# Layer-1 U gathers of a two-layer PEER trunk tied to TensorE steps, and input rows loaded once

## The chip, the cores and the metric

One core of one Trainium2 chip runs the whole program. The metric is device time in microseconds (us) of one execution, given as the median of several runs. PE is TensorE, PEld its weight loads, DVE is VectorE, ACT is ScalarE, POOL is GpSimd, and SP issues the plain DMAs.

## The reference

The program is a two-layer decoder trunk on 512 tokens of width 1024. Layer 0 mixes tokens with sliding-window attention, layer 1 with a short gated convolution. After each mixer comes a PEER block: a router picks 128 of 16384 experts for every token (8 heads, 16 each), and each expert is a row of U and a row of V.

```
h = rmsnorm(x, norm_mix[i]);  x = x + mixer_i(h)          # attention in layer 0, gated conv in layer 1
h = rmsnorm(x, norm_ffn[i]);  x = x + peer_ffn(h, ...)
# peer_ffn, for each token t and each of its 128 experts k:
u = take(expert_u, idx);  a = einsum('td,thkd->thk', h, u)
w = g * gelu(a)
v = take(expert_v, idx);  y = einsum('thk,thkd->td', w, v)
```

## The kernel before, in words

The 512 tokens are four tiles of 128. The PEER block is done in two ways at once. For tiles 0 and 1 the expert rows are **gathered**: `gather(l, t, r)` (lines 622 to 690) issues 128 indirect DMAs for the U rows (line 633, one 512 KB tile `ug` each, one expert of every token), VectorE multiplies each with the normalised tokens and sums it (line 638), and when all 128 sums are there, 128 indirect DMAs fetch the V rows (line 666, `vg`, one token each), which TensorE multiplies with the weights into `acc` (line 676). The buffers are six tiles of the pool `gp`, and two more in the second front (`GX1`, line 74). POOL issues these DMAs in order; one waits there until its buffer is free.

For tiles 2 and 3 the block is **dense**: `dense(l, rs, pool)` (lines 692 to 788) goes over all 128 groups of 128 experts. Step i has a U half, `ustep` (line 704): load `du`, split it into a high and a low part (`uh` on ACT, `ul` on DVE, lines 700 and 701), 24 matmuls by `mm3` into `psA`, GELU into `dw`; and a V half, `vstep` (line 714): multiply `dw` with the gate matrix G (line 717, on POOL while U rows are being gathered, else on DVE), split `dv` and `dw` (`vh`, `vl`, `wh`, `wl`), and 12 matmuls into `y` (line 735). U halves run 7 steps ahead, 15 of them before the first V half, so that the first and the last 8 V steps have no U half beside them. G is built 32 groups at a time from one-hot matrices by 16 calls of `gen` (lines 738 to 762: copies `jr`, `igr` on ACT, `oj`, `igr`, `oi` on DVE, 32 pairs of small matmuls `psG`).

A **front** is what comes ahead of the dense steps of a layer. The second front (layer 1) is: add the dense sums to the rows of tiles 2 and 3 (`finish`, line 790), norms and transposes of tiles 1 to 3, `conv` (line 352; 24 pieces of weights, each split into `whi` and `wlo` and followed by 24 matmuls into `psbcu`), the output projection `proj`, and `router` (16 weight pieces, matmuls `psrq` and `psrs`, then top-k selection in many small instructions on DVE). Then come 15 U halves and the first 16 calls of `gen`, called the preparation below.

Three generators write the program: `stream_d` (fronts and dense steps), `stream_g` (the four gathers: layer 0 tiles 0 and 1, layer 1 tiles 0 and 1) and `stream_f` (work of tiles 0 and 1 in the gaps). `merge` (line 814) takes from them by a clock of its own: each `yield` says how far its stream moves on, and `rate()` (line 806) gives that step for one gather from `FR0`, `FR1` (fronts) and `DR0`, `DR1` (dense steps; first number for U rows, second for V rows); a dense step counts `DSTEP` = 6.8. The order so written sets priorities, from which a scheduler fixes one order for each engine. `st["mark"]` names a matmul; a U gather that is written while it is set waits for that matmul on POOL (line 635). Before, it is set in the attention of tiles 1 to 3 alone and is removed afterwards.

```
def rate():
    u = 0 if st.get("gu") else 1
    if st["dense"]:
        return (DR1 if "f1" in st else DR0)[u]
    if st["front"]:
        return (FR1 if "f0" in st else FR0)[u]
    return GR0
```

The rows of x: tile 0 is loaded at line 112, tiles 1 to 3 for their norm in `attn_norm` (line 223, pool `b4`), and all four again at the end of `attn` (line 349, pool `l0`), for the residual.

Of the kernel before, what the change touches and what calls it, by code (L numbers as in the profile page):

```python
# [8 lines left out]
F32 = mybir.dt.float32  # L9
# [10 lines left out]
P = 128  # L20
D = 1024
KC = 8
S = 512
NT = 4
# [48 lines left out]
WSB = 2  # L73
GX1 = 2

DR0 = (2.4, 2.4)
DR1 = (2.5, 2.5)
FR0 = (2.2, 3.0)
FR1 = (3.0, 3.0)


@with_exitstack
def trunk(ctx: ExitStack, tc: tile.TileContext, a: dict, out: bass.AP):
    nc = tc.nc
# [3 lines left out]
    b4 = ctx.enter_context(tc.tile_pool(name="b4", bufs=BPB))  # L88
# [20 lines left out]
    xs = {}  # L109
    first = {}  # L110
# [63 lines left out]
    def mm3(ps, w, x, ts):  # L174
        for k in range(KC):
            nc.tensor.matmul(ps, w[0][:, k, :], x[0][:, k, ts], start=(k == 0), stop=False)  # L176
            nc.tensor.matmul(ps, w[0][:, k, :], x[1][:, k, ts], start=False, stop=False)  # L177
        for k in range(KC):
            nc.tensor.matmul(ps, w[1][:, k, :], x[0][:, k, ts], start=False, stop=(k == KC - 1))  # L179

    def proj(src, lhs, tiles, psum, sp):
        for h in range(2):
# [32 lines left out]
    def attn_norm(tiles, pool):  # L215
        gain = first.pop("gain", None) or gain_of(a["norm_mix"][0:1, :])
        res = []
        for t in tiles:
            if "x" in first:
                xs[t] = first.pop("x")  # L220
            else:
                xs[t] = b4.tile([P, D], F32, name="xq", tag="b4")
                nc.sync.dma_start(xs[t], a["x"][t * P:(t + 1) * P, :])
            hT = pool.tile([P, KC, P], F32, name="hTa", tag="hTa", bufs=4)
            normT(t, gain, hT, py)
            res.append(hT)
        return res
# [17 lines left out]
    def attn(tiles, qks, pool, L):  # L245
# [5 lines left out]
        for j, t in enumerate(tiles):  # L251
# [22 lines left out]
            ps = py("psk")  # L274
# [22 lines left out]
            for gp2 in range(2):  # L297
# [46 lines left out]
                nc.scalar.copy(oT[:, gp2], psov)  # L344
                if sp:
                    nc.vector.tensor_tensor(oL[:, gp2], psov, oT[:, gp2], op=ALU.subtract)
        for t in tiles:
            xs[t] = pool.tile([P, D], F32, name="x", tag="x", bufs=3)
            nc.sync.dma_start(xs[t], a["x"][t * P:(t + 1) * P, :])
        yield from proj(a["wo"], oTs, tiles, py, (pool, ("sc", "sc"), SCB) if sp else None)  # L350

    def conv(tiles, pool, psum, slow=1.0):
        n = len(tiles)
        T = n * P
# [36 lines left out]
        for c in range(KC):  # L391
            pss = [None] * 3
            cc = pool.tile([P, 3, T + 2], F32, name="cc", tag="cc")
            u, z, v = cc[:, 0, :T], cc[:, 1, :], cc[:, 2, :T]
            for part in (2, 1, 0):
                w = piece(a["w_in"][c, part])
                ps = psum(f"psbcu{part}")
                if c3:
                    mm3(ps[:, :T], split(w, pool, ("wh", "wl"), WSB), (hh, hl), slice(0, T))
                else:  # L400
                    for k in range(KC):
                        nc.tensor.matmul(ps[:, :T], w[:, k, :], hT[:, k, :], start=(k == 0), stop=(k == KC - 1))
                if part == 2:
                    nc.scalar.copy(u, ps[:, :T])
                elif part == 1:
                    nc.vector.tensor_copy(z[:, 0:2], zh[:, c, :])
                    nc.vector.tensor_tensor(z[:, 2:], ps[:, :T], u, op=ALU.mult)
                    nc.vector.tensor_copy(zh[:, c, :], z[:, T:T + 2])
                    nc.scalar.mul(v, z[:, 0:T], convw[:, 0, c:c + 1])
                    for q in (1, 2):  # L410
                        nc.vector.scalar_tensor_tensor(v, z[:, q:T + q], convw[:, q, c:c + 1], v,
                                                       op0=ALU.mult, op1=ALU.add)
                else:
                    y = v if sp else yT[:, c, :]
                    nc.vector.tensor_tensor(y, v, ps[:, :T], op=ALU.mult)
                    if sp:
                        nc.scalar.copy(yh[:, c, :], y)
                        nc.vector.tensor_tensor(yl[:, c, :], y, yh[:, c, :], op=ALU.subtract)
                yield 1.75 * n * slow
# [202 lines left out]
    def gather(l, t, r):  # L622
# [5 lines left out]
        for s in range(P):  # L628
            if early and s % TK == 0:
# [2 lines left out]
            ug = gtile("ug")  # L632
            ld = nc.gpsimd.indirect_dma_start(out=ug, out_offset=None, in_=a[f"u{l}"],  # L633
                                              in_offset=bass.IndirectOffsetOnAxis(ap=r["idx"][h][:, c:c + 1], axis=0))
            if "mark" in st:
                tc.add_manual_dep(ld.ins, st["mark"], together, reason="pace of the front")
            with tc.high_priority(offset=HPT):
                nc.vector.tensor_tensor_reduce(out=ug, in0=ug, in1=xn, scale=1.0, scalar=0.0, op0=ALU.mult,  # L638
# [53 lines left out]
    def dense(l, rs, pool):  # L692
# [21 lines left out]
        def vstep(i):  # L714
# [17 lines left out]
            for k, (x, m) in enumerate(terms):  # L732
                for tt in range(2):
                    for h in range(2):
                        nc.tensor.matmul(ys[tt][h], x[:, tt * P:(tt + 1) * P], m[:, h * 512:(h + 1) * 512],  # L735
                                         start=first and k == 0, stop=last and k == len(terms) - 1)

        def gen(i, tg):
            ijg = rs[tg * TG // P]["ijg"]
# [29 lines left out]
                gen(c * IC, tg)  # L769

        npre = GR - IC
        for i in range(LAG + npre):
            ustep(i)
            yield 1.0
# [3 lines left out]
        for i in range(NK):  # L778
# [7 lines left out]
            vstep(i)  # L786
            yield DSTEP
        st["ys"] = ys

    def finish(l, ys, pool):  # L790
        for tt in range(2):
# [70 lines left out]
    def stream_d():  # L862
        with tc.tile_pool(name="l0", bufs=1) as l0:
# [28 lines left out]
            def run(g):  # L892
                for v in g:
                    if isinstance(v, list):
                        return v
                    yield v
            hTs = attn_norm([0], l0)
            yield 5.0
            qk0 = yield from run(attn_qkv([0], hTs, l0, L, py, piece, 1.75))
            hTs = attn_norm([1, 2, 3], l0)  # L900
# [92 lines left out]
```

## Time and profile before

| what | value |
|---|---|
| median of 3 runs | 2992.05 us (2991.13 to 2999.46) |
| the profiled execution, its own time | 2989.34 us |
| its span, first to last instruction | 2987.5 us |
| busy, share of the span | PE 88%, PEld 70%, DVE 75%, ACT 52%, POOL 46% |
| mean granted TensorE clock | 0.943 |
| moved by DMA | 931.37 MB, mean 312 GB/s |

The 40 slices of the page, 75 us each, show the stages; each digit is the busy share in tenths. Counted from 0, the second front begins in slice 22 and the dense V steps of layer 1 in slice 28.

```profile
PE   5966878869999988999998699986788699999999
...
DVE  2496699984898899546479995988999946546655
...
POOL 0152554464555545434357754446755755541000
PEclk8987889969999999999999799998899899999999
```

PE is the engine with the most work, and the shares differ from stage to stage: there are slices in which DVE is at 9 and PE at 6 to 8, and the last eight have PE at 9, DVE near 5 and POOL falling to 0, which is where the gathers have ended. Below, a stage is named by its window in us from the start of the span, and a dense step of layer 1 by its number from 0 to 127.

### The profile page before, as it was taken

The numbers are of one execution on the slowest core, as the hardware profiler recorded it, in microseconds if no ns is written. First come the engines' busy times: TensorE is split into PE (matmuls) and PEld (weight loads), VectorE is DVE, ScalarE is ACT, GpSimd is POOL, SyncE is SP. The second block draws the span as 40 slices with busy tenths as digits, with TensorE's granted clock in tenths as the row PEclk, the third lists the DMA queues.
The fourth block names the chain that finished last, engine by engine and source line by source line (L and its number), as shares of the span: only waits on it lengthen the run. The fifth ranks groups of instructions, "written<-read, shape, count | busy, mean of one in ns | idle before, by whom it ended". The sixth has DMA issues, their size and how long they took to land. (4 is left out here: it accounts for less than half of the span.)

```text
span 2987.5 us, 53454 instructions
## 1 busy us (share of the span) xinstructions
PE 2624.3 (88%) x19980; PEld 2098.1 (70%) x19980; DVE 2246.6 (75%) x5225; ACT 1559.3 (52%) x2384; POOL 1364.6 (46%) x1163
## 2 busy tenths in 40 slices
PE   5966878869999988999998699986788699999999
PEld 5763476626788877777777696763577577777898
DVE  2496699984898899546479995988999946546655
ACT  4226333584773367448343333358356538637644
POOL 0152554464555545434357754446755755541000
PEclk8987889969999999999999799998899899999999
DMA  5883788989999988999999998998999899996554
GB/s 199 291 315 127 253 311 316 338 315 347 333 367 377 395 304 321 340 324 333 337 366 378 364 366 315 320 335 318 357 348 357 309 338 327 345 333 231 175 187 159
DMA packets 263203, 931.37 MB, mean 312 GB/s; under 512 B 29984, under 2 KB 38560, under 8 KB 262944
## 3 DMA queue, kind: packets, MB, share of 16 engines
q0 software_dynamic: 147456, 536.94, 49.5%
q1 hardware_dynamic: 115488, 391.03, 35.9%
q8 instruction: 157, 2.57, 0.3%
q14 instruction: 102, 0.84, 0.1%
HBM read 916.31 MB, written 11.53 MB: 311 GB/s over the span
## 5 line engine op out<-in xcount | busy, mean ns | idle before, releaser
L633 POOL DMA_INDIRECT ug<-in_u_dram,idx x512 | 684.7, 1337 | 669.6 <-DVE act L638 248.9
L666 POOL DMA_INDIRECT vg<-in_v_dram,idxT x512 | 553.7, 1081 | 640.1 <-PE acc L676 511.8
L638 DVE CUSTOM_DVE_ANT_0 ug<-ug,xn 128x1024 f32<-128x1024 f32 x512 | 626.0, 1235 | 40.0 <-DMA ug<-in_u_dram,idx 39.4
L176 PE MATMUL psA<-xh,uh 128*128 128x256 f32 x2048 | 523.4, 292 | 46.7 <-ACT dw L711 20.0
L177 PE MATMUL psA<-xl,uh 128*128 128x256 f32 x2048 | 510.9, 286 | 0.0
L701 DVE TENSOR_TENSOR ul<-du,uh 128x1024 fp32r<-128x1024 f32 x256 | 320.8, 1253 | 202.7 <-ACT uh L700 163.1
L176 PEld LDWEIGHTS psA<-xh,uh 128*128 128x128 f32 x2048 | 395.4, 193 | 104.9 <-ACT dw L711 32.7
L701 DVE TENSOR_TENSOR vl<-dv,vh 128x1024 fp32r<-128x1024 f32 x256 | 318.5, 1245 | 170.1 <-ACT vh L700 166.6
L177 PEld LDWEIGHTS psA<-xl,uh 128*128 128x128 f32 x2048 | 395.9, 193 | 16.4 <-issue 10.5
L700 ACT CAST uh<-du 128x1024 fp32r<-128x1024 f32 x256 | 268.7, 1050 | 204.7 <-PE psA L177 162.4
L700 ACT CAST vh<-dv 128x1024 fp32r<-128x1024 f32 x256 | 268.9, 1051 | 186.5 <-PE y L735 172.9
L676 PE MATMUL acc<-vg,wd 128*32 128x512 f32 x2048 | 290.4, 646 | 35.4 <-DMA vg<-in_v_dram,idxT 32.1
L179 PE MATMUL psA<-xh,ul 128*128 128x256 f32 x2048 | 299.0, 287 | 18.7 <-DVE ul L701 18.7
L735 PE MATMUL y<-vh,wh 128*128 128x512 f32 x1024 | 289.9, 403 | 27.0 <-ACT vh L700 18.4
L179 PEld LDWEIGHTS psA<-xh,ul 128*128 128x128 f32 x2048 | 266.7, 191 | 52.5 <-DVE ul L701 24.7
L735 PE MATMUL y<-vl,wh 128*128 128x512 f32 x1024 | 287.5, 402 | 16.0 <-DVE vl L701 15.7
L735 PE MATMUL y<-vh,wl 128*128 128x512 f32 x1024 | 283.2, 397 | 16.6 <-DVE wl L724 16.5
L742 ACT COPY jr<-ijg 128x2048 f16<-128x2048 f16 x128 | 243.5, 1902 | 50.6 <-DVE oj L746 49.7
L735 PEld LDWEIGHTS y<-vh,wl 128*128 128x128 f32 x1024 | 192.8, 190 | 73.1 <-DVE wl L724 20.8
L735 PEld LDWEIGHTS y<-vl,wh 128*128 128x128 f32 x1024 | 189.1, 191 | 72.4 <-DVE vl L701 21.2
L735 PEld LDWEIGHTS y<-vh,wh 128*128 128x128 f32 x1024 | 178.6, 191 | 73.8 <-ACT vh L700 25.6
L744 ACT COPY igr<-ijg 128x1536 f16<-128x1536 f16 x128 | 188.8, 1475 | 35.3 <-DVE oi L751 34.9
(208 smaller groups left out, 4004.8 us busy)
## 6 DMA issues: line engine op xcount, KB each, us to landing
du<-in_uT_dram SPq DMA_DIRECT2D x256, 512.0 KB, 6.5
dv<-in_v_dram SPq DMA_DIRECT2D x256, 512.0 KB, 6.3
wpc<-in_wq_dram SPq DMA_DIRECT2D x64, 512.0 KB, 6.0
wpc<-in_w_in_dram SPq DMA_DIRECT2D x48, 512.0 KB, 7.1
wpo<-in_wo_dram SPq DMA_DIRECT2D x16, 512.0 KB, 4.5
ug<-in_u_dram,idx POOLq DMA_INDIRECT x512, 7.6
vg<-in_v_dram,idxT POOLq DMA_INDIRECT x512, 7.2
wpo<-in_w_out_dram SPq DMA_DIRECT2D x16, 512.0 KB, 6.7
```

The lines of the kernel that those rows point to most:

```text
L176: nc.tensor.matmul(ps, w[0][:, k, :], x[0][:, k, ts], start=(k == 0), stop=False)
L177: nc.tensor.matmul(ps, w[0][:, k, :], x[1][:, k, ts], start=False, stop=False)
L179: nc.tensor.matmul(ps, w[1][:, k, :], x[0][:, k, ts], start=False, stop=(k == KC - 1))
L633: ld = nc.gpsimd.indirect_dma_start(out=ug, out_offset=None, in_=a[f"u{l}"], in_offset=bass.IndirectOffsetOnAxis(ap=r["idx"][h][:, c:c + 1 ...
L638: nc.vector.tensor_tensor_reduce(out=ug, in0=ug, in1=xn, scale=1.0, scalar=0.0, op0=ALU.mult, op1=ALU.add, accum_out=act[:, s:s + 1])
L666: ld = nc.gpsimd.indirect_dma_start(out=vg, out_offset=None, in_=a[f"v{l}"], in_offset=bass.IndirectOffsetOnAxis(ap=idxT[:, tt:tt + 1], ax ...
L676: mm = nc.tensor.matmul(acc[c:c + 32, :], wd[:, j, r8, :], vgs[j][:, h * 512:(h + 1) * 512], start=(q == 0 and r8 == 0), stop=(q == 3 and ...
L700: nc.scalar.copy(hi, w)
L701: nc.vector.tensor_tensor(lo, w, hi, op=ALU.subtract)
L735: nc.tensor.matmul(ys[tt][h], x[:, tt * P:(tt + 1) * P], m[:, h * 512:(h + 1) * 512], start=first and k == 0, stop=last and k == len(terms ...
L742: nc.scalar.copy(jr, ijg[:, 0, t0:t0 + TG].unsqueeze(2).to_broadcast([P, TG, P]))
L744: nc.scalar.copy(igr, ijg[:, 1:4, t0:t0 + TG].unsqueeze(3).to_broadcast([P, 3, TG, IC]))
```

## The change

**Holds.** `mm3` returns the name of its last matmul. In the `conv` of tiles 1 to 3, `st["mark"]` becomes the last matmul of each weight piece; a U gather of layer 1 written after it waits for it. In `dense(1)` the mark is the last matmul of the V step before the one written last (`st["next"]` carries it). At the beginning of a `dense` it is cleared, so that nothing is held in layer 0's dense steps and the V gathers never are.

**Numbers of the clock.** A U gather of the second front counts 3.5 and a V gather 2.5 (3.0 and 3.0 before). In the dense steps of layer 1 a U gather stays at 2.5 and a V gather counts 1.8 (2.5 before).

**Input rows.** Tiles 1 to 3 are loaded once, right after the norm of tile 0, into the pool `l0`, where they stay for the residual; tile 0 alone is loaded a second time, into `b4`. That makes 5 loads of 512 KB for x where there were 8.

```diff
@@ -74,9 +74,9 @@
 GX1 = 2
 
 DR0 = (2.4, 2.4)
-DR1 = (2.5, 2.5)
+DR1 = (2.5, 1.8)
 FR0 = (2.2, 3.0)
-FR1 = (3.0, 3.0)
+FR1 = (3.5, 2.5)
 
 
 @with_exitstack
@@ -176,7 +176,8 @@
             nc.tensor.matmul(ps, w[0][:, k, :], x[0][:, k, ts], start=(k == 0), stop=False)
             nc.tensor.matmul(ps, w[0][:, k, :], x[1][:, k, ts], start=False, stop=False)
         for k in range(KC):
-            nc.tensor.matmul(ps, w[1][:, k, :], x[0][:, k, ts], start=False, stop=(k == KC - 1))
+            mm = nc.tensor.matmul(ps, w[1][:, k, :], x[0][:, k, ts], start=False, stop=(k == KC - 1))
+        return mm.ins.name
 
     def proj(src, lhs, tiles, psum, sp):
         for h in range(2):
@@ -216,11 +217,8 @@
         gain = first.pop("gain", None) or gain_of(a["norm_mix"][0:1, :])
         res = []
         for t in tiles:
-            if "x" in first:
+            if t == 0:
                 xs[t] = first.pop("x")
-            else:
-                xs[t] = b4.tile([P, D], F32, name="xq", tag="b4")
-                nc.sync.dma_start(xs[t], a["x"][t * P:(t + 1) * P, :])
             hT = pool.tile([P, KC, P], F32, name="hTa", tag="hTa", bufs=4)
             normT(t, gain, hT, py)
             res.append(hT)
@@ -344,9 +342,9 @@
                 nc.scalar.copy(oT[:, gp2], psov)
                 if sp:
                     nc.vector.tensor_tensor(oL[:, gp2], psov, oT[:, gp2], op=ALU.subtract)
-        for t in tiles:
-            xs[t] = pool.tile([P, D], F32, name="x", tag="x", bufs=3)
-            nc.sync.dma_start(xs[t], a["x"][t * P:(t + 1) * P, :])
+        if tiles == [0]:
+            xs[0] = b4.tile([P, D], F32, name="x0", tag="b4")
+            nc.sync.dma_start(xs[0], a["x"][0:P, :])
         yield from proj(a["wo"], oTs, tiles, py, (pool, ("sc", "sc"), SCB) if sp else None)
 
     def conv(tiles, pool, psum, slow=1.0):
@@ -396,7 +394,7 @@
                 w = piece(a["w_in"][c, part])
                 ps = psum(f"psbcu{part}")
                 if c3:
-                    mm3(ps[:, :T], split(w, pool, ("wh", "wl"), WSB), (hh, hl), slice(0, T))
+                    st["mark"] = mm3(ps[:, :T], split(w, pool, ("wh", "wl"), WSB), (hh, hl), slice(0, T))
                 else:
                     for k in range(KC):
                         nc.tensor.matmul(ps[:, :T], w[:, k, :], hT[:, k, :], start=(k == 0), stop=(k == KC - 1))
@@ -632,7 +630,7 @@
             ug = gtile("ug")
             ld = nc.gpsimd.indirect_dma_start(out=ug, out_offset=None, in_=a[f"u{l}"],
                                               in_offset=bass.IndirectOffsetOnAxis(ap=r["idx"][h][:, c:c + 1], axis=0))
-            if "mark" in st:
+            if st.get("mark"):
                 tc.add_manual_dep(ld.ins, st["mark"], together, reason="pace of the front")
             with tc.high_priority(offset=HPT):
                 nc.vector.tensor_tensor_reduce(out=ug, in0=ug, in1=xn, scale=1.0, scalar=0.0, op0=ALU.mult,
@@ -732,8 +730,10 @@
             for k, (x, m) in enumerate(terms):
                 for tt in range(2):
                     for h in range(2):
-                        nc.tensor.matmul(ys[tt][h], x[:, tt * P:(tt + 1) * P], m[:, h * 512:(h + 1) * 512],
-                                         start=first and k == 0, stop=last and k == len(terms) - 1)
+                        mm = nc.tensor.matmul(ys[tt][h], x[:, tt * P:(tt + 1) * P], m[:, h * 512:(h + 1) * 512],
+                                              start=first and k == 0, stop=last and k == len(terms) - 1)
+            if l == 1:
+                st["mark"], st["next"] = st["next"], mm.ins.name
 
         def gen(i, tg):
             ijg = rs[tg * TG // P]["ijg"]
@@ -769,6 +769,7 @@
                 gen(c * IC, tg)
 
         npre = GR - IC
+        st["mark"] = st["next"] = None
         for i in range(LAG + npre):
             ustep(i)
             yield 1.0
@@ -786,6 +787,7 @@
             vstep(i)
             yield DSTEP
         st["ys"] = ys
+        st["mark"] = st["next"]
 
     def finish(l, ys, pool):
         for tt in range(2):
@@ -895,6 +897,9 @@
                         return v
                     yield v
             hTs = attn_norm([0], l0)
+            for t in range(1, NT):
+                xs[t] = l0.tile([P, D], F32, name="x", tag="x", bufs=3)
+                nc.sync.dma_start(xs[t], a["x"][t * P:(t + 1) * P, :])
             yield 5.0
             qk0 = yield from run(attn_qkv([0], hTs, l0, L, py, piece, 1.75))
             hTs = attn_norm([1, 2, 3], l0)
```

The built programs show where instructions stand now. **VectorE at the beginning of the second front**, between the last V step of layer 0 and the convolution (`xdn`: dense sums added to the rows; `nr`, `h`: the norm; `ug,act`: one U gather consumed). Before:

```order
L798 TENSOR_TENSOR xdn<-xdn,y_4527 128x512
L798 TENSOR_TENSOR xdn<-xdn,y_4528 128x512
L137 TENSOR_SCALAR nr<-nss 128x1
L638 ISA ug,act<-ug,xn 128x1024
L638 ISA act 128x1
L137 TENSOR_SCALAR nr<-nss 128x1
L139 RECIPROCAL nr<-nr 128x1
L146 SCALAR_TENSOR_TENSOR h<-x,nr,gain 128x1024
```

Now:

```order
L800 TENSOR_TENSOR xdn<-xdn,y_4521 128x512
L800 TENSOR_TENSOR xdn<-xdn,y_4522 128x512
L137 TENSOR_SCALAR nr<-nss 128x1 x2
L139 RECIPROCAL nr<-nr 128x1
L146 SCALAR_TENSOR_TENSOR h<-x,nr,gain 128x1024
L139 RECIPROCAL nr<-nr 128x1
L146 SCALAR_TENSOR_TENSOR h<-xdn,nr,gain 128x1024
L379 TENSOR_TENSOR hl<-psT,hh 128x4x128 x2
```

The U gathers are gone from between the steps of the norm. Counted over the whole order of VectorE: of the 128 U gathers of layer 1, tile 0, 39 are consumed before the last V steps of layer 0, none from there to the convolution, 35 in the convolution and 54 after it (15 in the projection, 39 in the router).

**VectorE in the router of the second front** (`wlo`: weights split; `i16u`, `rsc`, `cand`, `sel`: top-k). Before, no U gather stands there:

```order
L171 TENSOR_TENSOR wlo<-wpc,whi 128x1024
L432 MAX v_18748<-rsc 128x8 x2
L432 MAX v_18781<-rsc 128x8 x2
L434 MAX_INDEX i16u<-v_18748,rsc 128x8 x2
L457 TENSOR_TENSOR cand<-v_18748 128x48
```

Now:

```order
L171 TENSOR_TENSOR wlo<-wpc,whi 128x1024
L430 MAX gs<-cand 128x8
L432 MAX_INDEX i16u<-v_19073,rsc 128x8 x2
L432 MAX_INDEX i16u<-v_19103,rsc 128x8 x2
L636 ISA ug,act<-ug,xn 128x1024
L636 ISA act 128x1
L432 MAX_INDEX sel<-gs,cand 128x8
```

U gathers stand among the top-k instructions and the weight splits of the first two thirds of the router. The V gathers of tile 0 follow: 96 of the 128 are multiplied before the first V step of layer 1 (all of them before) and 32 in steps 0 to 13.

**POOL in the dense steps of layer 1** (`vg` ahead: tile 0; `ug`: tile 1; `dw`: line 717). Before:

```order
L666 DMA vg<-in_v_dram,idxT 128x1024 x10
L633 DMA ug<-in_u_dram,idx 128x1024 x6
L658 MEMSET wd 128x512
L633 DMA ug<-in_u_dram,idx 128x1024 x115
L717 TENSOR_TENSOR dw<-dw,G 128x256 x9
L633 DMA ug<-in_u_dram,idx 128x1024 x7
L717 TENSOR_TENSOR dw<-dw,G 128x256
```

Now, at the beginning and at the end of the same 128 gathers:

```order
L664 DMA vg<-in_v_dram,idxT 128x1024 x10
L656 MEMSET wd 128x512
L715 TENSOR_TENSOR dw<-dw,G 128x256 x5
L631 DMA ug<-in_u_dram,idx 128x1024
L715 TENSOR_TENSOR dw<-dw,G 128x256 x2
L631 DMA ug<-in_u_dram,idx 128x1024 x17
L715 TENSOR_TENSOR dw<-dw,G 128x256 x6
```

```order
L631 DMA ug<-in_u_dram,idx 128x1024 x22
L715 TENSOR_TENSOR dw<-dw,G 128x256 x8
L631 DMA ug<-in_u_dram,idx 128x1024 x18
L664 DMA vg<-in_v_dram,idxT 128x1024 x22
```

The first U gather of tile 1 is held to V step 23 and the last to step 70, 2 or 3 to a step. On VectorE they stand from step 25 to step 74 (0 to 37 before), and on TensorE the V gathers of tile 1 stand from step 73 to step 120 (38 to 83 before).

## Rows read from the trace of the kernel before

**Rows 1.** Page, part 1: busy time and share of the span, by engine.

```profile
PE 2624.3 (88%) x19980; PEld 2098.1 (70%) x19980; DVE 2246.6 (75%) x5225; ACT 1559.3 (52%) x2384; POOL 1364.6 (46%) x1163
```

**Rows 2.** Busy time by stage, second front and dense steps; the first line names the columns.

```profile
core 0: us, PE busy (x) PEld busy (x) DVE busy (x) ACT busy (x) POOL busy (x), PEclk, DMA share, GB/s
1646.00:1675.00 29.00, 6.06 (x26) 4.71 (x24) 27.13 (x49) 9.92 (x17) 19.60 (x16) 0.59 0.98 376
1675.00:1783.00 108.00, 104.58 (x579) 103.69 (x578) 107.18 (x182) 35.56 (x47) 75.41 (x55) 0.95 0.97 370
1783.00:2090.00 307.00, 265.41 (x2329) 190.18 (x2327) 247.85 (x1027) 170.93 (x253) 151.00 (x143) 0.94 0.89 322
2090.00:2169.40 79.40, 59.68 (x279) 47.50 (x280) 78.11 (x135) 29.61 (x40) 55.47 (x39) 0.86 0.93 358
2169.40:2259.90 90.50, 75.72 (x637) 64.24 (x636) 88.27 (x134) 55.23 (x72) 52.33 (x37) 0.98 0.95 349
2259.90:2651.10 391.20, 357.40 (x2910) 275.18 (x2913) 265.83 (x337) 228.62 (x297) 231.93 (x202) 0.97 0.92 333
2651.10:2957.00 305.90, 302.22 (x2330) 259.45 (x2331) 180.41 (x232) 177.83 (x253) 23.41 (x24) 0.99 0.63 214
```

**Rows 3.** Windows of line 638 alone: DVE busy (two instructions per gather), clock, DMA.

```profile
1646.00:1675.00 29.00, 16.44 (x29) 0.59 0.98 376
1675.00:1783.00 108.00, 64.16 (x108) 0.95 0.97 370
1783.00:2090.00 307.00, 11.05 (x18) 0.94 0.89 322
2077.00:2390.00 313.00, 156.84 (x256) 0.92 0.92 341
```

**Rows 4.** Waits of PE in 0 to 24 and in 1646 to 1675 us.

```profile
PE psq L237 <- DMA wpc<-in_wqkv_dram: 4.7, 2, 4.3
...
PE psT L377 <- DVE h L146: 22.9, 3, 16.0
```

**Rows 5.** Groups by line: busy us and mean ns of one, idle time and its releaser.

```profile
L633 POOL DMA_INDIRECT ug<-in_u_dram,idx x512 | 684.7, 1337 | 669.6 <-DVE act L638 248.9 <-DVE i16u L434 141.1 <-issue 63.6
L701 DVE TENSOR_TENSOR ul<-du,uh 128x1024 fp32r<-128x1024 f32 x256 | 320.8, 1253 | 202.7 <-ACT uh L700 163.1 <-issue 35.8 <-ACT dw L711 2.4
L676 PE MATMUL acc<-vg,wd 128*32 128x512 f32 x2048 | 290.4, 646 | 35.4 <-DMA vg<-in_v_dram,idxT 32.1 <-DVE wd L659 2.1 <-issue 1.2
L701 DVE TENSOR_TENSOR vl<-dv,vh 128x1024 fp32r<-128x1024 f32 x256 | 318.5, 1245 | 170.1 <-ACT vh L700 166.6 <-issue 2.3 <-PE psT L153 0.7
L746 DVE TENSOR_TENSOR oj<-jr,io 128x2048 f16<-128x2048 f16 x128 | 157.1, 1227 | 37.1 <-PE psG L755 26.3 <-ACT jr L742 7.2 <-ACT uh L700 1.9
L755 PE MATMUL psG<-oi,oj 128*128 128x32 f16 x4096 | 128.5, 178 | 35.8 <-DVE oi L751 26.5 <-ACT G L762 9.2
L724 DVE TENSOR_TENSOR wl<-dw,wh 128x256 fp32r<-128x256 f32 x240 | 103.7, 432 | 28.7 <-ACT wh L723 28.3
L751 DVE TENSOR_TENSOR oi<-igr 128x1024 f16<-128x1024 f16 x128 | 91.6, 716 | 0.7
L749 DVE TENSOR_TENSOR igr<-igr,io 128x512 f16<-128x512 f16 x128 | 57.2, 446 | 31.7 <-ACT igr L744 30.8
```

**Rows 6.** DMA issues, 1675 to 1783 and 2100 to 2360 us: count, median us to landing.

```profile
ug<-in_u_dram,idx POOLq DMA_INDIRECT x49, 8.0
...
ug<-in_u_dram,idx POOLq DMA_INDIRECT x113, 7.6
```

**Rows 7.** Windows of line 666 alone: POOL busy (one instruction per V gather).

```profile
1816.00:2077.00 261.00, 132.24 (x121) 0.93 0.91 330
2716.00:2957.00 241.00, 1.15 (x1) 0.99 0.54 181
```

**Rows 8.** Chain that ended last: start, us, what; V steps 20 apart.

```profile
2819.70 2.77 PE y L735 x12
...
2931.84 2.77 PE y L735 x12
```

## The prediction, made before the change was run

> **What bounds the kernel now.** I read the page's busy shares first [rows 1], then the busy time stage by stage [rows 2]. PE has the most work, 88% of the span, but the stage windows show two kinds of stage. In the convolution (1675 to 1783 us) and in the first dense steps of layer 1 (2090 to 2260 us) VectorE is busy 97 to 99% of the time, and in those dense steps PE only 75 to 84%: there VectorE ends last. In the last 306 us it is the reverse: PE 302 us, VectorE 180 us, the DMA engines at 0.63. The windows of line 638 say why [rows 3]: U gathers take 64 of VectorE's 107 us in the convolution, 16 of 27 us in the norms ahead of it, and 157 us in 2077 to 2390. After 2716 us a single V gather is left [rows 7], and a dense step takes (2931.84 - 2819.70) / 20 = 5.61 us [rows 8], PE's own pace. So the gathers crowd the front and the first third of the dense steps, and the last third has none. The change moves both groups later. The question at each place is what VectorE or PE has there already.
>
> **The change, part by part.** The sum is made against the profiled execution, 2989.34 us. One U gather costs VectorE 156.84 / 128 = 1.225 us [rows 3]. One V gather costs PE 290.4 / 512 = 0.567 us, and one call of `gen` costs VectorE 1.227 + 0.446 + 0.716 = 2.389 us and PE 128.5 / 128 = 1.0 us [rows 5].
>
> *Start.* Three row tiles, 1.57 MB, now go ahead of the first weights on SP's queue. At the 322 GB/s of 1783 to 2090 us [rows 2] that is 4.9 us. They no longer stand ahead of the second batch of weights, for which PE waited 4.3 us [rows 4]. Between +4.9 and -4.3 I take 0. The loads saved later were hidden behind the attention.
>
> *Norms, 29 us.* PE waited 22.9 us for the norm [rows 4], VectorE being at U gathers for 16.4 us [rows 3]. None stands there now. What is left is 27.1 - 16.4 = 10.7 us of VectorE and 6.1 us of PE, one after the other, so 18 us with ACT in between: **-11** (ends -16 and -6).
>
> *Convolution, 108 us.* VectorE falls to 107.2 - 64.2 + 35 x 1.225 = 86 us, and PE's 104.6 us come next. A held gather issues in 1.34 us [rows 5], lands in 8.0 us [rows 6], is summed in 1.23 us, and ahead of the next split (1.25 us) and its last third of a piece (1.5 us); that chain of 13.3 us runs over three pieces, which take 3 x 108 / 24 = 13.5 us. It does not bind, but nearly. I take 105 us: **-3** (ends -3 and, with landings of 10 us, +14).
>
> *Projection, router, preparation, 307 us.* VectorE was busy 247.85 us, 11.05 of them U gathers. Now 54 U gathers stand there: 247.85 - 11.05 + 54 x 1.225 = 303 us. At 97.5%, the lower of its two shares in 2090 to 2260 us [rows 2], this takes 311 us: **+4**. PE's 265 us lose 32 V gathers, 18 us, and hide behind it. The low end is 100% busy, -4. The high end is the V gathers' chain, +24, below.
>
> *V steps 0 to 12, 79.4 us.* The first eight have no U half: 8 x 2.77 + 5 x 5.61 = 50 us of PE [rows 8], and 32 V gathers add 18 us. At the pace of 261 / 121 = 2.16 us for a V gather [rows 7] the 32 take 69 us. I take 72: **-7**.
>
> *Steps 13 to 23, 90.5 us.* The hold keeps all U gathers out: 11 x 5.61 + 7 calls of `gen` x 1.0 = 69 us: **-22**. PE alone, nothing else is near.
>
> *Steps 24 to 71, 391.2 us.* Here stand the 128 U gathers, 2 or 3 to a step. VectorE: 48 x (1.253 + 1.245 + 0.432) = 141 us for the splits [rows 5], 157 us for the gathers, 25 calls of `gen` x 2.389 = 60 us, together 357 us, at 97.5% 366 us. At step 64 the first `dw` of a new group of 32 stands on POOL behind the last three held gathers, 3 x 1.34 = 4 us. So 370 us: **-21** (ends -34, VectorE never idle, and 0). PE would need 294 us, so VectorE is still the bound, only over more steps.
>
> *Steps 72 to 119, 305.9 us.* All 128 V gathers of tile 1 now fall here: 48 x 5.61 + 128 x 0.567 + 13 x 1.0 = 355 us: **+49**. PE was full here and stays full, so this is paid in full. The last eight steps stay as they are.
>
> *The holds themselves.* A held gather reaches VectorE 1.34 + 7.6 = 8.9 us after its matmul at the earliest [rows 5, 6]. In VectorE's order 85 of the 128 stand two V steps behind their hold (over 11.2 us, enough), but 39 stand one step behind, some 14 steps' worth. A step of 370 / 48 = 7.7 us leaves 1.2 us each, 17 us in all; at 5.61 us it would be 3.3 us each, 46 us. VectorE has other work of the step ahead of most of them. Between 0 and 46 I take **+5**, near the low end, since VectorE is behind anyhow in these steps.
>
> Here the Trainium skill says otherwise: "DMA: Bandwidth & Descriptors", section "Anatomy of one DMA — SWDGE (gpsimd) path", puts such a transfer at 2.0 us plus its bytes at 436 GB/s, an estimate of 3.2 us for 512 KB. By that the holds would cost nothing and the sum would be 5 us lower. The rows have 7.6 and 8.0 us with the queues full [rows 6], so I go by the rows.
>
> Sum: 0 - 11 - 3 + 4 - 7 - 22 - 21 + 49 + 5 = **-6 us**, 2983 us for the profiled execution. The median of the runs lay 2.7 us above that execution, so the forecast is **2986 us**: what the front and the early steps win, the late steps give back, since the same gathers meet a VectorE that is nearly full again and a PE that is full. About 0.3%, 9 us, is what a measurement of this kernel can tell from no change; 2986 is within it.
>
> **The rivals.**
>
> *VectorE packs fully (faster, 2960 us).* If it idles nowhere in 1783 to 2090 (-4 instead of +4) and in steps 24 to 71 (-34 instead of -21), and the holds cost nothing (0 instead of +5), the sum is -32. For: 98% in steps 0 to 12 [rows 2]. Against: top-k in the router waits for PE's scores, and VectorE was at 81% there. Chance 0.26.
>
> *The clock (faster, 2968 us).* The granted clock was 0.94 in 1783 to 2090 and 0.86 in steps 0 to 12 [rows 2], between the levels of 1.2 and 2.4 GHz, with PE waiting in both. If the gaps close and PE runs at the full level, its 265 and 60 busy us shrink by 16 and 8. PE ends last in only part of these stages, so some 18 us more. Chance 0.12.
>
> *The holds bind (slower, 3017 us).* With landings of 9.0 us instead of 7.6, the 39 gathers that stand one step behind lack 2.6 us even in 7.7 us steps, 14 x 2.6 = 36 us instead of 5. Behind a waiting gather on VectorE stand the splits of the next step, and PE waits for those. For: 8.0 us was measured in the convolution [rows 6]. Against: fewer gathers are in flight at a time now. It decides from about 8.5 us. Chance 0.17.
>
> *The V gathers come too late (slower, 3006 us).* 54 U gathers after the convolution, at the 2.0 us of the convolution (54 in 108 us, [rows 3]), end near 1769 + 108 = 1877 us; then 96 V gathers must be multiplied before the first V step, 8 of them fetched ahead. At 2.16 us the 88 take 190 us, until about 2076, in time. At 2.5 us they take 220 us, the first V step comes at 2105 and +4 becomes +24. It decides from 2.3 us. Chance 0.10.
>
> *The change does not do what it says (2982 us).* If the U gathers come to POOL later than their holds anyway, the dense steps stay as they were (0 for all of them) and the front's -10 is all. Against: before, they were issued from 2077 us on, before step 0 [rows 3]. Chance 0.03.
>
> **How the numbers follow.** The forecast has 0.32, with a range of its own of 2975 to 2997 us. Faster by over 0.3%: 0.26 + 0.12 and a little of the rest, 0.40. Slower: 0.17 + 0.10 and a little, 0.28. Within: 0.32. The range reaches from below the first rival to the third, 2955 to 3018 us, and leaves out longer landings and a clock gain on top of full packing.
>
> **What would show it.** Right: norms near 18 us; VectorE over 95% from 1783 us to the first V step, which comes within 10 us of 2090 less the 14 us won; V steps 13 to 23 at about 6 us each; 24 to 71 at 7.7 us with VectorE at 97%; 72 to 119 at 7.4 us with PE full. Wrong: waits of VectorE for `ug` over 20 us in all, or of PE for `vg` before the first V step; steps 24 to 71 near 7.0 us or over 8.3; a first V step later than 2100 us.

## The result, and the profile after

3016.05 us (median of 4 runs, 3010.35 to 3019.13) against 2992.41 us for the kernel before, measured beside it: ratio 1.0072 (95% interval 1.0054 to 1.0090), slower by 0.7%. The forecast was 2986 us, 0.2% faster than before and within the 0.3% that can't be told from no change. The range, 2955 to 3018 us, holds the time, but the time moved the other way.

The page's first part answers to [rows 1]:

```profile
PE 2627.6 (87%) x19980; PEld 2097.5 (70%) x19980; DVE 2256.1 (75%) x5225; ACT 1557.9 (52%) x2383; POOL 1378.5 (46%) x1163
```

The work is the same; what changed is when it is done. Busy time by stage, to lay beside [rows 2]: norms, convolution, projection, norm of the router, router, U halves of the preparation, its calls of `gen`, then V steps 0 to 12, 13 to 23, 24 to 71 and 72 to 119.

```profile
core 0: us, PE busy (x) PEld busy (x) DVE busy (x) ACT busy (x) POOL busy (x), PEclk, DMA share, GB/s
1644.00:1665.00 21.00, 5.65 (x26) 4.86 (x25) 12.34 (x20) 9.45 (x17) 0.00 (x0) 0.61 0.40 150
1665.00:1768.00 103.00, 102.36 (x575) 100.71 (x575) 82.11 (x135) 35.23 (x47) 43.73 (x34) 0.98 0.79 276
1768.00:1805.00 37.00, 34.37 (x148) 27.04 (x147) 34.91 (x53) 9.31 (x10) 30.16 (x20) 1.00 0.99 381
1805.00:1828.00 23.00, 5.88 (x28) 5.08 (x26) 20.91 (x35) 9.21 (x16) 15.13 (x12) 0.66 0.96 385
1828.00:1951.00 123.00, 109.06 (x849) 93.88 (x847) 119.00 (x542) 41.15 (x98) 73.01 (x58) 0.93 0.88 311
1951.00:2011.00 60.00, 51.69 (x389) 38.59 (x389) 54.72 (x252) 32.74 (x50) 27.58 (x25) 0.97 0.94 344
2011.00:2110.00 99.00, 58.46 (x769) 28.17 (x768) 71.64 (x249) 73.54 (x73) 53.58 (x49) 0.75 0.82 287
2110.50:2182.20 71.70, 70.96 (x430) 47.31 (x431) 34.73 (x54) 31.82 (x42) 27.70 (x28) 0.96 0.88 322
2182.20:2253.80 71.60, 70.43 (x665) 62.07 (x664) 50.91 (x61) 58.32 (x80) 6.71 (x6) 1.00 0.50 168
2253.80:2622.70 368.90, 312.86 (x2499) 272.44 (x2497) 348.51 (x475) 222.41 (x289) 242.91 (x173) 0.96 0.87 317
2622.70:2984.10 361.40, 357.85 (x2724) 266.78 (x2723) 187.88 (x246) 180.58 (x257) 135.90 (x132) 1.00 0.92 332
```

Every row but those from 1768 to 2110 us lies near its forecast. Those five make 342 us where 307 were before and 311 forecast. The same stage of the kernel before, cut at the end of the router:

```profile
1783.00:1953.00 170.00, 162.27 (x1174) 121.20 (x1172) 124.55 (x541) 64.52 (x130) 77.27 (x77) 0.98 0.89 318
1953.00:2090.00 137.00, 103.14 (x1157) 68.98 (x1156) 123.30 (x487) 106.40 (x123) 73.73 (x66) 0.88 0.90 326
```

The first part, projection and router, went from 170 to 183 us, with VectorE busy 174.8 us (96%) where it had been 124.6 (73%). The second, the preparation, went from 137 to 159 us although VectorE is busy there about as long as before, 126 us (123). Line 636, the U sums, shows where VectorE's added time comes from (answering to [rows 3]):

```profile
1665.00:1768.00 103.00, 38.09 (x62) 0.98 0.79 276
1768.00:1828.00 60.00, 33.10 (x55) 0.87 0.98 383
1828.00:1951.00 123.00, 36.57 (x62) 0.93 0.88 311
```

69.7 us of them now lie behind the convolution, in whose own 103 us VectorE is left idle for 21. PE's waits in 1768 to 2110 us:

```profile
PE psG L755 <- DVE oi L751: 23.4, 9, 5.2
PE psT L153 <- DVE h L146: 17.1, 2, 9.4
...
PE psrq L563 <- ACT rsc L572: 7.3, 1, 7.3
...
PE acc L674 <- DMA vg<-in_v_dram,idxT: 3.2, 2, 2.8
```

The wait for the norm that the hold shortened ahead of the convolution stands again at the next norm (`psT <- h`), where U sums now are. PE hardly ever waits for a V row to land. Followed back from the first V step to the end of the convolution, from each wait to what ended it as in the page's fourth part, the chain of the kernel before spends 186 us on PE and 38 on VectorE, that of the changed one 108 on PE and 143 on VectorE. The chain doesn't tell the cost by itself: that of e3 below spends 184 us on VectorE and 90 on PE, and its front is shorter than the one before (437 us against 443).

### The profile page after: what moved, and what is told of

The parts are those of the page before. It is cut to its first block, busy times and chain, and to the rows that moved or that the text cites. A ratio compares the mean times of both kernels' runs of the same rounds, so it can differ in the third digit from the quotient of the medians.

```text
span 3014.3 us, 53432 instructions
## 1 busy us (share of the span) xinstructions
PE 2627.6 (87%) x19980; PEld 2097.5 (70%) x19980; DVE 2256.1 (75%) x5225; ACT 1557.9 (52%) x2383; POOL 1378.5 (46%) x1163
## 5 line engine op out<-in xcount | busy, mean ns | idle before, releaser
L636 DVE CUSTOM_DVE_ANT_0 ug<-ug,xn 128x1024 f32<-128x1024 f32 x512 | 633.6, 1248 | 52.6 <-DMA ug<-in_u_dram,idx 52.2
L746 DVE TENSOR_TENSOR oj<-jr,io 128x2048 f16<-128x2048 f16 x128 | 161.3, 1260 | 80.8 <-remote 25.9
```

The source lines that it names most:

```text
L746: nc.vector.tensor_tensor(oj, jr, io128.unsqueeze(1).to_broadcast([P, TG, P]), op=ALU.is_equal)
```

## The experiments

All ratios are to the kernel before, run beside them on the same chip. Front is the time from the end of layer 0's last V step to the first V step of layer 1, dense from there to the last one's end, in the profiled execution (us). Where one program was profiled twice (changed and e13, e5 and e14, e8 and e17, e9 and e15), the fronts agree within 1 us but for e5 and e14, the dense times within 7 us.

| kernel | ratio (95% interval) | front | dense |
|---|---|---|---|
| before | 1 | 443 | 892 |
| changed | 1.0072 (1.0054 to 1.0090) | 466 | 898 |
| e1 no front hold | 0.9983 (0.9970 to 0.9996) | 442 | 883 |
| e2 no dense holds | 1.0071 (1.0050 to 1.0091) | 451 | 904 |
| e3 old numbers | 0.9996 (0.9981 to 1.0011) | 437 | 886 |
| e4 no holds | 1.0000 (0.9987 to 1.0013) | 442 | 888 |
| e5 old front numbers | 1.0000 (0.9988 to 1.0013) | 440 | 904 |
| e6 short U sums | 0.9948 (0.9928 to 0.9967) | 423 | 906 |
| e7 half the V rows | 1.0042 (1.0027 to 1.0058) | 468 | 879 |
| e8 spread | 0.9915 (0.9900 to 0.9930) | 444 | 866 |
| e9 old U number | 1.0098 (1.0079 to 1.0117) | 449 | 917 |
| e10 U number 4.5 | 1.0097 (1.0079 to 1.0114) | 467 | 886 |
| e11 both, early | 1.0056 (1.0042 to 1.0070) | 490 | 875 |
| e12 spread more | 0.9988 (0.9978 to 0.9999) | 450 | 876 |
| e13 changed, again | 1.0096 (1.0080 to 1.0112) | 465 | 893 |
| e14 as e5 | 1.0053 (1.0040 to 1.0067) | 449 | 906 |
| e15 as e9 | 1.0089 (1.0068 to 1.0109) | 449 | 924 |
| e16 V number 3.0 | 1.0110 (1.0090 to 1.0130) | 468 | 906 |
| e17 as e8 | 0.9933 (0.9914 to 0.9952) | 444 | 868 |
| e18 numbers of e8 | 0.9979 (0.9965 to 0.9993) | 444 | 886 |

e1 to e4 ran on one chip, e5 to e8 on a second, e9 to e16 on a third, e17 and e18 on a fourth.

### Which part of the change

Theory A puts the loss down to the front hold, B to the dense holds and the V gathers that they push to the end, C to the new numbers.

e1, the front hold alone taken out:

```diff
-                    st["mark"] = mm3(ps[:, :T], split(w, pool, ("wh", "wl"), WSB), (hh, hl), slice(0, T))
+                    mm3(ps[:, :T], split(w, pool, ("wh", "wl"), WSB), (hh, hl), slice(0, T))
```

> The changed kernel without its holds in the convolution; holds in the dense steps, numbers and input rows as changed. Theory A (the held front loads the router and the preparation, where VectorE or the chain behind it binds): the first V step of layer 1 comes near 2090 us as before, the dense steps stay at about 900 us, total 2994 us (2988 to 3000). Theory B (the holds in the dense steps and the V gathers that they push to the end cost the 24 us): the total stays near 3012 us. Theory C (neither hold, but the new numbers of the clock): near 3014 us.

e2, the dense holds alone taken out:

```diff
-            if l == 1:
-                st["mark"], st["next"] = st["next"], mm.ins.name
```

> The changed kernel without its holds in the dense steps; holds in the convolution, numbers and input rows as changed. Theory A: the first V step still comes near 2110 us, the dense steps take some 892 us as before, total 3008 us (3002 to 3016). Theory B: near 2994 us. Theory C: near 3014 us.

e3, the numbers alone put back:

```diff
-DR1 = (2.5, 1.8)
+DR1 = (2.5, 2.5)
-FR1 = (3.5, 2.5)
+FR1 = (3.0, 3.0)
```

> Both holds and the input rows as changed, the four numbers of the clock as before (U and V gathers of the second front 3.0, V gathers of the dense steps 2.5). Theory A: still some 21 us late at the first V step, total near 3016 us (3008 to 3022). Theory B: near 3016 us. Theory C: near 2993 us.

e4, the edits of e1 and e2 together:

> Neither hold; the new numbers and the input rows as changed. Theories A and B: as the kernel before, 2990 us (2984 to 2997), first V step near 2088 us. Theory C: near 3014 us.

With neither hold the numbers and the input rows change nothing (1.0000). With these numbers, the dense holds alone gain a little (e1), and the front hold alone costs the whole loss (e2): B falls. For e3, A expected 3016 us and C 2993; 2986.3 came, so both holds with the old numbers cost nothing on this chip. The loss takes the front hold and the new numbers together, and A and C are each half right. In e1, the stage behind the convolution up to the end of the router, the preparation, and V steps 0 to 12:

```profile
1794.00:1961.00 167.00, 161.26 (x1174) 121.11 (x1173) 123.76 (x541) 62.70 (x127) 78.36 (x76) 0.99 0.88 311
1961.00:2094.00 133.00, 104.30 (x1159) 68.76 (x1158) 120.93 (x481) 103.55 (x120) 66.87 (x60) 0.87 0.89 320
2094.00:2150.00 56.00, 52.98 (x280) 45.52 (x280) 35.21 (x54) 32.51 (x45) 0.45 (x1) 0.94 0.49 162
```

Both parts are back (167 and 133 us), and V steps 0 to 12 have no V gather left: 56 us instead of 72.

### VectorE or the stream of gathers

Two theories for the front. D: VectorE, filled by the U sums, sets the time. S: the stream of gathers does, one 512 KB block of rows after the other.

e5:

```diff
-FR1 = (3.5, 2.5)
+FR1 = (3.0, 3.0)
```

> The changed kernel with 3.0 and 3.0 for a gather in the second front, as before; V gathers of the dense steps stay at 1.8, both holds stay. It parts the two pairs of numbers: if the 3.5 and 2.5 of the front cost the time when the front is held, the first V step comes near 2086 us as with all old numbers, and the total is 2990 us (2984 to 2998); if the 1.8 of the dense steps costs it, the first V step stays near 2105 us and the total near 3012 us.

e6, the last 54 U sums over 64 of their 1024 columns:

```diff
-                nc.vector.tensor_tensor_reduce(out=ug, in0=ug, in1=xn, scale=1.0, scalar=0.0, op0=ALU.mult,
+                e = 64 if (l, t) == (1, 0) and s >= 74 else D
+                nc.vector.tensor_tensor_reduce(out=ug[:, :e], in0=ug[:, :e], in1=xn[:, :e], scale=1.0, scalar=0.0, op0=ALU.mult,
```

> The changed kernel, but the last 54 U sums of layer 1, tile 0 (those after the convolution) run over 64 columns instead of 1024; every gather is still fetched. Theory D (VectorE, loaded by the U sums, sets the time from the end of the convolution to the first V step): VectorE falls there from 301 to about 240 us, the stretch from 342 to about 305 us, total 2975 us. Theory S (the stream of gathers sets it: 55 U and 102 V rows of 512 KB, one after the other at about 2.2 us, with the DMA engines at 0.9): the stretch stays at 325 to 342 us, total 3000 to 3016 us.

e7, every second V gather left out (`vg` and `ld` of j = 0 kept for j = 1):

```diff
-                        vg = gtile("vg")
+                        if j == 0 or (l, t) != (1, 0):
+                            vg = gtile("vg")
...
```

> The changed kernel, but of every pair of V gathers of layer 1, tile 0 only the first is fetched and both matmul groups use it: 64 transfers of 512 KB fewer, the work of VectorE and TensorE the same. Theory S: the stream ends some 51 transfers of 2.2 us sooner, the stretch from the convolution to the first V step falls from 342 us until VectorE's 301 us bind, 305 to 315 us, V steps 0 to 12 from 72 to about 60 us, total 2965 to 2980 us. Theory D: the stretch stays at 330 to 342 us, total 2995 to 3010 us.

e5 gives 440 us and 1.0000: it is the front's pair of numbers, not the 1.8 of the dense steps. e6, the two parts of the stage:

```profile
1760.00:1916.00 156.00, 136.30 (x952) 120.07 (x954) 122.67 (x626) 58.69 (x123) 76.26 (x73) 0.93 0.90 335
1916.00:2054.00 138.00, 105.60 (x1171) 66.52 (x1163) 127.34 (x506) 105.60 (x123) 73.91 (x65) 0.86 0.90 328
```

Some 52 us of VectorE less, and the first part takes 156 us instead of 183. The stage takes 294 us where D expected about 305. But every U row was still fetched at the old pace (1.96 us apart, 1.94 in the changed kernel), and the first V multiply came 130 us behind the convolution, 134 in the changed kernel. What fell with the edit is the number of V multiplies that PE's order has ahead of the first V step, 76 instead of 96; 15 of the 20 are missing in the first part. The second part shrinks too, 159 to 138 us, though no U sum stands in it. e7:

```profile
1758.00:1976.00 218.00, 183.64 (x1295) 130.24 (x1294) 185.92 (x678) 64.17 (x130) 137.08 (x115) 0.93 0.91 335
1976.00:2102.70 126.70, 83.22 (x1037) 67.71 (x1036) 118.65 (x450) 106.17 (x123) 11.54 (x12) 0.83 0.41 148
```

With 64 transfers fewer, the DMA engines at 0.41 in the preparation, the first V step still comes 344 us behind the convolution, as D expected. But the order changed with this edit too: in e7 PE multiplies 98 V rows in the router instead of 28, and that part grows by 35 us; 30 instead of 68 stand in the preparation, and that shrinks by 32. All 128 stand ahead of the first V step, and the last of them begins 88 us ahead of it; the preparation, with VectorE busy 118.65 of 126.7 us, ends last. So e7 doesn't refute S. The V multiplies between the convolution and the first V step, four matmuls for a row, from the first start to the last; before, changed, e6, e7:

```profile
L676 PE MATMUL acc<-vg,wd x512: 589/617/1064, 1820.5 to 2083.2; 128*32 128x512 f32 x171
L674 PE MATMUL acc<-vg,wd x384: 589/617/1063, 1902.7 to 2104.4; 128*32 128x512 f32 x192
L675 PE MATMUL acc<-vg,wd x304: 589/617/1063, 1889.6 to 2053.1; 128*32 128x512 f32 x152
L675 PE MATMUL acc<-vg,wd x512: 589/592/617, 1893.0 to 2014.7; 128*32 128x512 f32 x171
```

The same counted in the other profiles; times are from the convolution's last matmul, and "each" is the time from the first V multiply to the first V step, divided by their number:

| kernel | first V multiply, us | V multiplies | each, us | first V step, us |
|---|---|---|---|---|
| before | 37 | 128 | 2.10 | 307 |
| changed; e13 | 134; 134 | 96 | 2.16; 2.18 | 342; 343 |
| e1 | 35 | 128 | 2.07 | 300 |
| e2 | 135 | 96 | 2.02 | 328 |
| e3 | 119 | 96 | 2.03 | 314 |
| e5; e14 | 119; 119 | 96 | 2.07; 2.16 | 317; 327 |
| e6 | 130 | 76 | 2.16 | 294 |
| e8 | 35 | 128 | 2.08 | 301 |
| e10 | 148 | 92 | 2.14 | 345 |
| e11 | 105 | 128 | 2.00 | 361 |
| e12 | 34 | 128 | 2.13 | 307 |

In all of these the last V multiply ends 0 to 6 us ahead of the first V step, and a V row takes 2.0 to 2.2 us, in e6 with 52 us less on VectorE as in the changed kernel. So two counts tell the front's length: when the U sums are done, since a V row is multiplied only then, and how many V rows are ordered ahead of the first V step. The front hold puts 57 U sums behind the convolution, 2.1 us apart where VectorE needs 1.2 for one; this moves the first V multiply by 97 us. 32 V rows fewer stand ahead, which gives back 62 us (128 x 2.10 against 96 x 2.16). Together that is the +35 us. With the old numbers 51 U sums stand behind the convolution (e3, e5; 52 in e14), and the first V multiply comes 15 us sooner; that is what the front's pair of numbers is worth here.

D falls for the time at which the U sums are done, which moved by 4 us in e6. Whether the scheduler put 20 V rows fewer ahead there because VectorE had less to do isn't shown. What sets the 2.1 us for a V row, of which PE is busy 0.567 us [rows 5], isn't settled. For S: in e7 the V gathers still go out 2.2 us apart (64 from 1866.5 to 2002.5 us), and the multiplies, two to a gather, come 0.96 us apart. Against it: in the changed kernel PE waits 3.2 us in all for V rows to land, while POOL waits for PE to free their buffers, so PE's fixed order may set the pace as well:

```profile
POOL vg L664 <- PE acc L674: 88.3, 34, 11.7
```

e9 and e10, the U number alone:

```diff
-FR1 = (3.5, 2.5)
+FR1 = (3.0, 2.5)     # e9
+FR1 = (4.5, 2.5)     # e10
```

> The changed kernel with the U number of the second front alone back at 3.0 (V gathers stay at 2.5, both holds, dense numbers as changed). In VectorE's order 52 instead of 48 U sums of tile 0 stand in the convolution and 37 instead of 41 behind it. If the U number is what costs the time: front (layer 0's last V step to layer 1's first) near 440 us, total 2990 us (2984 to 2998). If the V number is: front 451 to 466 us, total 3005 to 3016 us.

> The changed kernel with the U number of the second front at 4.5: 41 U sums in the convolution and 49 behind it. Theory D: each of the 8 costs at least its 1.2 us on VectorE behind the convolution, so front 465 to 480 us and total 3025 us or more (3015 to 3045). If the number of U sums behind the convolution doesn't matter: total 3005 to 3016 us as with 3.5.

e11, both holds with `FR1 = (2.0, 2.0)` and `DR1 = (3.2, 1.8)`:

> Both holds, but numbers that let the U sums into the convolution and spread the dense ones: 2.0 and 2.0 in the second front, 3.2 and 1.8 in the dense steps. 60 U sums stand in the convolution and 28 behind it, those of tile 1 from V step 0 on. Theory D: the norm keeps its 12 us gain and less is given back behind the convolution, front 420 to 432 us, dense steps 865 to 875 us, total 2945 us (2935 to 2958). If the held front costs by itself, however its sums are placed: front 440 us or more, total 2962 us or more.

e9 missed by itself: the front shrank to 449 us, but the dense steps lost it again (917). e10 came out at 1.0097, no worse than the changed kernel's repeat on the same chip (1.0096): its first V multiply comes 14 us later, but 4 V rows fewer stand ahead of the first V step, and each took 2.14 us instead of 2.18. e11 is the clearest miss: the fewest U sums of the four kernels stand behind the convolution (43 in the trace; 51 in e9, 57 in the changed kernel, 65 in e10, where the expectations count 28, 37, 41 and 49), and the front is the longest of all, since all 128 V multiplies stand ahead of the first V step, 98 of them in the preparation:

```profile
1773.60:1938.00 164.40, 147.06 (x1022) 123.64 (x1022) 157.06 (x593) 59.47 (x123) 93.20 (x76) 0.93 0.92 326
1938.00:2135.00 197.00, 131.21 (x1284) 73.56 (x1282) 140.08 (x517) 112.33 (x130) 105.76 (x105) 0.79 0.85 308
```

The first part is as short as without a hold, and the second takes 64 us more than in e1, which has the same 128 V rows ahead but begins them 70 us sooner after the convolution. VectorE is busy 297 us in e11's stage of 361 us, and 301 in the changed kernel's of 342: VectorE's load, D's measure, doesn't tell the time.

### The pairs of numbers on one chip

> The changed kernel itself, beside the next three on one chip: ratio to the kernel before 1.007 (1.005 to 1.010). If the first measurement owed part of its loss to its chip, 1.004 or less.

> 3.0 and 3.0 in the second front, everything else as changed. If the pair costs the held front its time: ratio 1.000 (0.998 to 1.002). If the earlier difference was the chips': within 0.002 of the changed kernel's ratio here.

> 3.0 and 2.5 in the second front. If the U number costs it (four U sums fewer behind the convolution): near 1.000. If the V number does: near the changed kernel's ratio, 1.007 to 1.010.

e16, `FR1 = (3.5, 3.0)`:

> 3.5 and 3.0 in the second front. If the V number costs it: near 1.000. If the U number does: near 1.007.

The pair put back wins 0.43% (1.0096 to 1.0053), either number alone nothing that the intervals tell. The U number sets the front (465 and 468 us with 3.5 and 57 U sums behind the convolution, 449 with 3.0 and 51 or 52), but the sums of tile 1 then come in an order in which steps 24 to 71 take 386 (e14) and 396 us (e15) instead of 363 (e13). Which feature of that order costs them wasn't pursued. On this chip the kernel with both holds and the pair back still loses 0.5% (e14), on the second chip nothing (e5).

### A version that beats both

e8, no front hold, dense holds kept:

```diff
-DR1 = (2.5, 1.8)
+DR1 = (3.2, 1.8)
-FR1 = (3.5, 2.5)
+FR1 = (2.5, 2.0)
...
-                    st["mark"] = mm3(ps[:, :T], split(w, pool, ("wh", "wl"), WSB), (hh, hl), slice(0, T))
+                    mm3(ps[:, :T], split(w, pool, ("wh", "wl"), WSB), (hh, hl), slice(0, T))
```

> No hold in the convolution, the holds in the dense steps kept, and numbers that let the U gathers of tile 1 begin near V step 10 and stand 2 to a step: 2.5 and 2.0 in the second front, 3.2 and 1.8 in the dense steps. By theories D and S alike the front is as before (first V step 442 us behind layer 0's last V step), and the dense steps, 883 us with the holds at step 23, lose the empty stretch without gathers: 24 to 71 falls from 372 to about 345 us and the V gathers begin sooner; total 2965 us (2955 to 2980). If spreading gains nothing because V steps 13 to 23 grow by what the later ones lose: 2983 us.

e12, the same with `FR1 = (2.3, 1.9)` and `DR1 = (3.8, 1.5)`:

> No hold in the convolution, dense holds kept, U sums of tile 1 from about V step 6 on and 1.8 to a step (2.3 and 1.9 in the second front, 3.8 and 1.5 in the dense steps). If VectorE in the dense steps is what is left: 24 to 71 falls from 351 to about 340 us, total 2957 us (2950 to 2965). If the V gathers, which then come closer together at the end (4.5 to a step), bind by their transfers: the last steps grow by 10 us or more, total 2965 to 2980 us.

> The spread version once more, beside the next: ratio 0.9915 (0.989 to 0.994) if its gain is its own; 0.996 or more if the chip of its first measurement gave it part of that.

e18, e8 without its dense holds:

> The numbers of the spread version without any hold. U sums of tile 1 then stand as in the kernel before, from the preparation to V step 35. If the holds make the gain: ratio 1.000 (0.997 to 1.003). If the numbers alone do: 0.992.

V steps 0 to 12, 13 to 23, 24 to 71 and 72 to 119 of e8:

```profile
2090.00:2144.00 54.00, 52.13 (x284) 44.16 (x281) 33.98 (x51) 32.42 (x44) 12.51 (x10) 0.98 0.58 189
2144.00:2222.60 78.60, 72.34 (x622) 63.21 (x620) 73.77 (x97) 50.94 (x71) 48.05 (x34) 0.98 0.87 305
2222.60:2573.30 350.70, 308.95 (x2530) 272.35 (x2529) 320.22 (x434) 227.49 (x294) 190.10 (x145) 0.95 0.83 296
2573.30:2930.80 357.50, 356.54 (x2716) 266.66 (x2715) 187.85 (x245) 178.46 (x254) 130.60 (x132) 1.00 0.94 335
```

Two sums to a step from step 10 on leave VectorE busy 320 of 351 us in 24 to 71, and V steps 13 to 23 take only 8 us more than in e1. 0.9915 and, on another chip, 0.9933: medians 26 and 18 us under the kernel before. Its numbers without holds give 0.9979, so the holds make most of it. e12, spread further, ran on the third chip, where e5's kernel did worse too; whether it is worse than e8 can't be told from that.

## Why the prediction was wrong, point by point

- *Start* (0): -2. *Norms* (-11): -8, 21 us instead of 18. *Convolution* (-3): -5, with PE busy 102.4 of 103 us; the chain of 13.3 us did not bind.
- **The step that failed** is "Projection, router, preparation": "VectorE was busy 247.85 us ... At 97.5% ... this takes 311 us: +4". Measured +35. VectorE's work was right, 34.9 + 20.9 + 119.0 + 54.7 + 71.6 = 301 us against 303. The share was wrong, 88%, since VectorE's total doesn't tell the stage's time (e11). The rows account for it: the first V multiply came 134 us behind the convolution instead of 37, then 96 rows at 2.16 us instead of 128 at 2.10. The term hid PE's 32 rows fewer behind VectorE and left the start of the rows to a rival. That rival, "The V gathers come too late" (0.10), had the mechanism, the place and nearly the number (first V step at 2105 us, measured 2110), though not the sizes: it called 2.16 us a row in time and put the delay down to 2.5. At 2.16 us they came late, because the U sums ended at 1891 us and not at 1877, the first multiply followed at 1903, and 96 rows, not 88, came after it. (Its own terms, 1877 + 190 and 1877 + 220, make 2067 and 2097 us, not 2076 and 2105.) One sign of being wrong came true, a first V step later than 2100 us; the other of that place, waits of PE for `vg`, came to 3.2 us.
- *V steps 0 to 12* (-7): -8. *13 to 23* (-22): -19, all PE. *24 to 71* (-21): -22, VectorE 348.5 of 368.9 us, 94% where 97 were expected. *72 to 119* (+49): +55; PE 357.9 us against 355. The dense steps together: +4 forecast, +6.5 measured, so the argument that early and late steps cancel held.
- *The holds themselves* (+5): VectorE waited 12.1 us for `ug` in 24 to 71 (14 waits, longest 1.5), part of it hidden. In e1, which has the same holds and numbers in the dense steps:

```profile
DVE ug L636 <- DMA ug<-in_u_dram,idx: 16.3, 14, 3.2
```

```profile
ug<-in_u_dram,idx POOLq DMA_INDIRECT x128, 8.0
```

The 8.0 us to landing bear out the rows that were taken (7.6 and 8.0), and "The holds bind" did not come true: 24 to 71 are no longer than forecast. The Trainium skill, "DMA: Bandwidth & Descriptors", section "Anatomy of one DMA — SWDGE (gpsimd) path", would have put such a landing at an estimated 3.2 us and the holds at nothing; the trace disagrees with it by 4.8 us a transfer.
- "VectorE packs fully" and "The clock" fell: VectorE was at 88% from 1768 us to the first V step, and the granted clock in the calls of `gen` was 0.75, with PE busy 58 of 99 us, where it had been 0.88, with PE busy 65 of 91 us.

## What to carry to other kernels

Set moved work against the stretch in which it lands, cut at each change of the bounding engine, and not against a whole stage: spare time later in the stage doesn't take it up. Then follow what can start only when the moved work is done, and count it at its measured pace: here the V rows began 97 us later, and leaving 32 of them for the steps behind gave back only 62. An engine that is 96% busy where the moved work lands needn't be what ends last: e6 took 52 us off VectorE, and the V rows began 4 us sooner. A hold is worth what its released work finds: ahead of the router one lost 0.7%, in steps with room the other kind is most of a gain of 0.7 to 0.9%.

## What the runs showed of the hardware that was not expected

One and the same program (e5 and e14) came out at 1.0000 of the kernel before on one chip and at 1.0053 on another (intervals 0.9988 to 1.0013 and 1.0040 to 1.0067), each against the kernel before on its own chip. The first V multiply came 119 us behind the convolution in both; the 96 V rows then took 2.07 us each on the one and 2.16 on the other, 9 us in all, by which the fronts differ. The profile of the second shows waits that end with nothing recorded that would end them (`remote`); the first has none:

```profile
ACT whi L170 <- remote: 9.8, 2, 5.7
...
ACT G L762 <- remote: 6.5, 3, 2.9
...
DVE oj L746 <- remote: 6.0, 4, 2.0
```

The changed kernel's two profiles have such waits too. They come with a gap in the record: e14's trace holds 1783 of the 1884 updates of PE's semaphore, e5's holds all, so these lines say nothing of a cause. Why a V row takes longer on that chip stays open. Comparisons of half a per cent should be made on one chip; there e9 and e15, one program too, came out at 1.0098 and 1.0089.
